# Order of the moving columns and start addresses of the matmul operands in a two-layer encoder kernel

## Chip, cores and metric

The kernel runs on one NeuronCore of one Trainium2 chip. The metric is the device time of one execution in microseconds. Two executions of the kernel before the change took 1149.13 and 1155.57 us; their median is 1152.35 us.

## What is computed

The reference is a bidirectional encoder of two layers on one sequence of 256 tokens with 1024 channels, all in float32. One layer, with the parts that this case does not touch left out:

```python
h = x + 0.5 * swiglu(rms_norm(x, norm_ffn1[i]), w_ffn1_in[i], w_ffn1_out[i])     # 1024 -> 2 x 2816 -> 1024
u = rms_norm(h, norm_mix[i])
q, k, v, c, g = jnp.split(u @ w_in[i], splits, axis=-1)                           # 512, 128, 128, 1024, 2048
y_attn = window_attention(q, k, v, sink[i], rel_bias) @ w_attn_out[i]
...
y_conv = c @ w_conv_out[i]
g_attn, g_conv = jnp.split(jax.nn.sigmoid(g), 2, axis=-1)
h = h + (g_attn * y_attn + g_conv * y_conv) @ w_o[i]
h = h + 0.5 * swiglu(rms_norm(h, norm_ffn2[i]), w_ffn2_in[i], w_ffn2_out[i])
x = h + (p[i] @ w_pe_proj[i]) * jax.nn.sigmoid(rms_norm(h, norm_pe[i]) @ w_pe_gate[i])
```

Nearly all of the arithmetic is in the matrix products with the weights. The rms norms scale each token, so the kernel multiplies the unscaled activations with the weights and scales the product afterwards.

## The kernel before

**Layout.** Activations are kept with channels on the 128 partitions and the 256 tokens along the free dimension: an activation of 1024 channels is a tile `[128, 8, 256]`, one row of 256 tokens (1024 bytes of a partition) for each group `k` of 128 channels. The result of a product is again channels by tokens, so that the weights are the stationary operand (128 x 128, loaded by a LDWEIGHTS, row "PEld" in the profile) and the 256 tokens are the moving one.

**Three products for one.** To keep float32 accuracy with the `float32r` type of the matmul, each operand is held as a pair: a part `hi`, rounded to `float32r`, and a part `lo`, what the rounding left. `mm3` (lines 309 to 317) adds three matmuls for each `k` into one PSUM tile: weight hi by activation hi (line 315), weight hi by activation lo (line 316), weight lo by activation hi (line 317). Each is one LDWEIGHTS of 128 columns and one matmul of 256 columns. `mm3` serves every product with a weight but five: keys and values (lines 676 to 678) and queries (lines 720 to 722) have it the other way round, with 128 tokens of `u` as the stationary operand and 256 or 512 columns of the weight tile as the moving one; the two output projections of attention and convolution (line 852) are plain float32 matmuls, each of which shows as two records in the trace; attention itself has its own.

**Weights.** `Weights` loads blocks of up to 1 MB from HBM into four buffers `raw` (SP's queue, line 76), and cuts them into pieces of at most 128 x 1024. For each piece ScalarE writes `w_hi` (line 100) and VectorE writes `w_lo` (line 101). Both come from one pool, `w_pool` (line 145), with seven buffers each, and `get` prepares up to six pieces ahead (line 132).

**Where things lie.** Pools lie behind one another in each partition of SBUF in the order of their creation: constants, the raw buffers, the weight tiles, a gap of 64 bytes (`gap0`, line 146), the activations (`xp`), temporary tiles, another gap of 64 bytes, and then, opened and closed as the layers go, the pool of a feed-forward stage or of the mixer. All tiles of the weight pool are 4096 bytes and those of the activations are 8192 or 22528, all multiples of 256. In the laid-out program all fourteen weight tiles begin at a multiple of 256 bytes and all activations that `mm3` reads (`x`, `xe`, `h`, `ym`, the transposed `p`) begin 64 bytes beyond one. `new_x` (line 341) makes the pair of an activation; it is reused under the tags `xah` and `xal`, so that x0, xm0, xf0, xn0, xm1 and xf1 stand in the same place one after the other.

**Order of the work.** For each layer `l`, in order: `ffn` (first feed-forward; `gate_up` 22 times, PSUM tile `ps_gu`, moving operand x; then `down` eight times, `ps_fo`, moving operand `h`), `mix` (`conv_in`, `ps_c`; keys and values, `ps_kv`; queries, `ps_q`; `conv_in` again; `gates`, `ps_g`, moving operand xm; attention, put between the gates; `attn_out` and `conv_out`, `ps_ao` and `ps_co`; `mix_out`, `ps_wo`, moving operand `ym`), `ffn` again (moving operands xf and `h`), and `embed` (`ps_pp` and `ps_pe`, moving operand `xe`). The order of the instructions on each engine comes from the framework's scheduler, by priorities; the groups of one PSUM tile follow one another on TensorE, and their evacuations follow on VectorE and ScalarE a group later (`group`, `flush`).

## Time and profile before

| what | value |
|---|---|
| two executions | 1149.13 and 1155.57 us |
| span of the profiled execution | 1155.8 us |
| TensorE matmul busy | 98 % of the span |
| TensorE weight load busy | 95 % |
| VectorE, ScalarE, GpSimd busy | 70 %, 53 %, 8 % |
| DMA queue of SP | 201.60 MB, 52.9 % of 16 engines' time |
| granted TensorE clock | 1.000 |

The profiled execution is one more execution; its span of 1155.8 us is from the first to the last instruction, and no time from outside is given for it. It lies 3.4 us above the median of the two timed ones. Matmuls are pipelined: one of 256 columns lasts some 280 ns by its record while the next one begins after less than half of that. So "busy" tells only that TensorE always had a matmul under way. What counts is the **pitch**: the time from the start of one matmul to the start of the next. It is read from a timeline (two starts and the number of matmuls between them) or from a count of matmuls in a stretch of time. In a count by windows, a matmul that is under way at either edge is counted too, so that the pitch is the stretch plus the length of one record, divided by the count.

### The profile page before, as it was taken

How to read it: one execution, taken by the hardware profiler on the slowest of the kernel's cores; microseconds unless marked ns; L12 is line 12 of the kernel's file. 1: busy time of each engine (PE TensorE's matmuls, PEld its weight loads, DVE VectorE, ACT ScalarE, POOL GpSimd, SP SyncE). 2: the span in 40 equal slices, each digit the busy share in tenths (PEclk: the TensorE clock that was granted, in tenths of full speed). 3: DMA queues.
4: the chain of work that ended last, by engine and by line, in shares of the span. 5: the costliest groups of instructions: out<-in, count | busy, mean ns of one | idle time of the engine just before them, and what ended most of it. 6: DMA issues, size and time to landing. Idle time of an engine off the chain costs nothing.

```text
span 1155.8 us, 21813 instructions
## 1 busy us (share of the span) xinstructions
PE 1136.7 (98%) x9082; PEld 1100.9 (95%) x9082; DVE 812.1 (70%) x1214; ACT 610.4 (53%) x1029; POOL 88.8 (8%) x123
## 2 busy tenths in 40 slices
PE   7999999999989999999999999999999999999998
PEld 7999999998879999999999999999987899999997
DVE  5866656798767766656886666669986686666564
ACT  6644444676346544444664444457753564444443
POOL 3000001211002000001110000113000010000110
PEclk9999999999999999999999999999999999999999
DMA  8866556545074565546556464566522664644541
GB/s 256 265 236 213 170 176 208 182 149 138 8 254 157 187 215 168 179 166 219 188 177 204 162 207 156 171 218 197 143 77 65 227 228 152 214 163 149 200 147 37
DMA packets 195695, 203.00 MB, mean 176 GB/s; under 512 B 3731, under 2 KB 188899, under 8 KB 195596
## 3 DMA queue, kind: packets, MB, share of 16 engines
q1 hardware_dynamic: 195564, 201.60, 52.9%
q8 instruction: 71, 1.16, 0.4%
q14 instruction: 28, 0.23, 0.1%
q10 hardware_dynamic: 32, 0.01, 0.0%
HBM read 200.53 MB, written 1.06 MB: 174 GB/s over the span
## 4 chain that ended last, share of the span: by engine, by line
PE 95%; DMA 2%; DVE 2%; ACT 1%; issue 0%; SPq 0%; ACTq 0%; DVEq 0%
PE ps_gu L317 14%; PE ps_gu L315 14%; PE ps_gu L316 14%; PE ps_fo L315 7%; PE ps_fo L317 7%; PE ps_fo L316 7%; PE ps_g L315 3%; PE ps_g L317 3%; PE ps_g L316 3%; PE ps_ao L852 2%; DMA raw<-in_w_o_dram 2%; PE ps_s L760 1%; PE ps_wo L316 1%; PE ps_c L315 1%; PE ps_pe L317 1%; PE ps_c L317 1%
## 5 line engine op out<-in xcount | busy, mean ns | idle before, releaser
L101 DVE TENSOR_TENSOR w_lo<-raw,w_hi 128x1024 fp32r<-128x1024 f32 (+1 forms) x368 | 441.6, 1204 | 227.8 <-ACT w_hi L100 225.9
L100 ACT CAST w_hi<-raw 128x1024 fp32r<-128x1024 f32 (+1 forms) x368 | 377.8, 1032 | 411.6 <-PE ps_gu L316 207.5
L315 PE MATMUL ps_fo<-h_hi,w_hi 128*128 128x256 f32 x704 | 196.1, 279 | 0.0
L316 PE MATMUL ps_fo<-h_lo,w_hi 128*128 128x256 f32 x704 | 195.9, 279 | 0.0
L317 PE MATMUL ps_fo<-h_hi,w_lo 128*128 128x256 f32 x704 | 195.9, 279 | 0.0
L317 PEld LDWEIGHTS ps_fo<-h_hi,w_lo 128*128 128x128 f32 x704 | 131.8, 188 | 0.0
L315 PEld LDWEIGHTS ps_fo<-h_hi,w_hi 128*128 128x128 f32 x704 | 131.8, 188 | 0.0
L316 PEld LDWEIGHTS ps_fo<-h_lo,w_hi 128*128 128x128 f32 x704 | 131.7, 187 | 0.0
L404 POOL TENSOR_TENSOR sq_acc<-sq_acc,sq 128x256 f32<-128x256 f32 x56 | 56.9, 1015 | 887.0 <-ACT sq L403 886.5
L315 PE MATMUL ps_gu<-x0h,w_hi 128*128 128x256 f32 x352 | 99.4, 282 | 2.0 <-ACT x L460 2.0
L612 DVE SCALAR_TENSOR_TENSOR y<-cpad,cw,y 128x256 f32<-128x256 f32 x240 | 101.2, 477 | 0.1
L317 PE MATMUL ps_gu<-x0h,w_lo 128*128 128x256 f32 x352 | 99.4, 282 | 0.2 <-DVE w_lo L101 0.2
L316 PE MATMUL ps_gu<-x0l,w_hi 128*128 128x256 f32 x352 | 98.9, 281 | 0.0
L315 PE MATMUL ps_gu<-xf0h,w_hi 128*128 128x256 f32 x352 | 98.6, 280 | 0.0
L315 PE MATMUL ps_gu<-xf1h,w_hi 128*128 128x256 f32 x352 | 98.6, 280 | 0.0
L316 PE MATMUL ps_gu<-xn0l,w_hi 128*128 128x256 f32 x352 | 98.5, 280 | 0.0
L315 PE MATMUL ps_gu<-xn0h,w_hi 128*128 128x256 f32 x352 | 98.4, 280 | 0.0
L316 PE MATMUL ps_gu<-xf0l,w_hi 128*128 128x256 f32 x352 | 98.4, 280 | 0.0
L316 PE MATMUL ps_gu<-xf1l,w_hi 128*128 128x256 f32 x352 | 98.4, 280 | 0.0
L317 PE MATMUL ps_gu<-xf0h,w_lo 128*128 128x256 f32 x352 | 98.3, 279 | 0.0
L317 PE MATMUL ps_gu<-xf1h,w_lo 128*128 128x256 f32 x352 | 98.3, 279 | 0.0
L317 PE MATMUL ps_gu<-xn0h,w_lo 128*128 128x256 f32 x352 | 98.2, 279 | 0.0
(225 smaller groups left out, 2677.8 us busy)
## 6 DMA issues: line engine op xcount, KB each, us to landing
raw<-in_w_ffn_in_dram SPq DMA_DIRECT2D x86, 1024.0 KB
raw<-in_w_in_dram SPq DMA_DIRECT2D x30, 1024.0 KB
raw<-in_w_ffn_out_dram SPq DMA_DIRECT2D x32, 896.0 KB
raw<-in_w_ffn_out_dram SPq DMA_DIRECT2D x16, 1024.0 KB
raw<-in_w_o_dram SPq DMA_DIRECT2D x8, 1024.0 KB
raw<-in_w_pe_gate_dram SPq DMA_DIRECT2D x8, 1024.0 KB
raw<-in_w_attn_out_dram SPq DMA_DIRECT2D x8, 512.0 KB
raw<-in_w_conv_out_dram SPq DMA_DIRECT2D x4, 1024.0 KB
```

What stands on the lines that cost most here:

```text
L100: nc.scalar.copy(out=hv[:, :, d0 : d0 + w], in_=src),
L101: nc.vector.tensor_tensor(out=lv[:, :, d0 : d0 + w], in0=src, in1=hv[:, :, d0 : d0 + w].bitcast(F32), op=ALU.subtract,),
L315: nc.tensor.matmul(ps, wh[:, k0 + k, cols], xh[:, kx, :], start=f, stop=False)
L316: nc.tensor.matmul(ps, wh[:, k0 + k, cols], xl[:, kx, :], start=False, stop=False)
L317: nc.tensor.matmul(ps, wl[:, k0 + k, cols], xh[:, kx, :], start=False, stop=e)
L404: nc.gpsimd.tensor_tensor(out=self.acc, in0=self.acc, in1=sq, op=ALU.add)
L612: nc.vector.scalar_tensor_tensor(out=y[:, i, :], in0=src, scalar=w, in1=y[:, i, :], op0=ALU.mult, op1=ALU.add)
L760: nc.tensor.matmul(ps[:, c, :], qT[v * HD : (v + 1) * HD, c, qb * P : (qb + 1) * P], kT[v * HD : (v + 1) * HD, :], start=True, stop=True,)
L852: nc.tensor.matmul(ps[:, c * T : (c + 1) * T], w[:, k, c * P : (c + 1) * P], x[:, k, :], start=k == 0, stop=k == KC - 1,)
```

## The change

Two things are changed, both in what addresses TensorE reads and in what order.

**Order.** `mm3` passes the moving rows and the PSUM tile through a view, `order.cols`. The view `plain` leaves them as they are. The view `by_halves` takes the 256 columns as two halves of 128 and reads four columns of the first half, four of the second, the next four of the first, and so on; the result is written to PSUM in the same order, so each column lands where it did. The halves lie 512 bytes apart. `by_halves` is set in `down` of the first feed-forward of both layers, in `gate_up` of the second feed-forward of both layers, in the gates of layer 1 and in `mix_out` of layer 0. Everywhere else the order is plain.

**Addresses.** The weight tiles get pools of their own for hi and lo, and each tile is eight columns (32 bytes) longer than its data, so that the seven buffers of either begin at 0, 32, 64, 96, 128, 160 and 192 bytes modulo 256. Small gap tiles (32 bytes each) part the pools. An activation tile is eight columns longer too, and its data begin at 0, 2, 4 or 6 columns (0, 8, 16 or 24 bytes) into it: x0 at 0, xm0 at 2, xf0 at 0, xn0 at 4, xm1 at 0, xf1 at 4, `xe` at 6, `h` at 0, 2, 4 and 6 in the four feed-forward stages. By the sizes of the tiles, activations hi and lo begin 64 and 96 bytes beyond a multiple of 256 for x, and 128 and 160 for a tile pair at the start of a feed-forward's pool, plus these columns.

The number of instructions of every kind stays the same, but for two memsets of gap tiles at the start.

```diff
+W_STEP = 8
...
-            hi = self.w_pool.tile([P, KD * P], F32R, name="w_hi")
-            lo = self.w_pool.tile([P, KD * P], F32R, name="w_lo")
+            hi = self.hi_pool.tile([P, KD * P + W_STEP], F32R, name="w_hi")
+            lo = self.lo_pool.tile([P, KD * P + W_STEP], F32R, name="w_lo")
...
-    w_pool = ctx.enter_context(tc.tile_pool(name="w_pool", bufs=W_BUFS))
+    hi_pool = ctx.enter_context(tc.tile_pool(name="hi_pool", bufs=W_BUFS))
+    gap2 = ctx.enter_context(tc.tile_pool(name="gap2", bufs=1))
+    lo_pool = ctx.enter_context(tc.tile_pool(name="lo_pool", bufs=W_BUFS))
+    gap3 = ctx.enter_context(tc.tile_pool(name="gap3", bufs=1))
     gap0 = ctx.enter_context(tc.tile_pool(name="gap0", bufs=1))
...
+    for gap in (gap2, gap3):
+        nc.gpsimd.memset(gap.tile([P, W_STEP], F32, name="gap"), 0.0)
...
+    def by_halves(v):
+
+        return v.rearrange("p (b a c) -> p a b c", b=2, c=4)
...
     def mm3(ps, w, x, first=True, last=True, k0=0, x_k0=0, n_k=None, cols=slice(0, P)):
         (wh, wl), (xh, xl) = w, x
+        view = order.cols
+        ps = view(ps)
...
-            nc.tensor.matmul(ps, wh[:, k0 + k, cols], xh[:, kx, :], start=f, stop=False)
-            nc.tensor.matmul(ps, wh[:, k0 + k, cols], xl[:, kx, :], start=False, stop=False)
-            nc.tensor.matmul(ps, wl[:, k0 + k, cols], xh[:, kx, :], start=False, stop=e)
+            nc.tensor.matmul(ps, wh[:, k0 + k, cols], view(xh[:, kx, :]), start=f, stop=False)
+            nc.tensor.matmul(ps, wh[:, k0 + k, cols], view(xl[:, kx, :]), start=False, stop=False)
+            nc.tensor.matmul(ps, wl[:, k0 + k, cols], view(xh[:, kx, :]), start=False, stop=e)
...
-    def new_x(tag, name):
-        return (
-            xp.tile([P, KD, T], F32R, name=name + "h", tag=tag + "h"),
-            xp.tile([P, KD, T], F32R, name=name + "l", tag=tag + "l"),
-        )
+    def rows(pool, k, name, off, **kw):
+        t = pool.tile([P, k * T + 8], F32R, name=name, **kw)
+        return t[:, off : off + k * T].rearrange("p (k t) -> p k t", t=T)
+
+    def new_x(tag, name, off):
+        return tuple(rows(xp, KD, name + part, off, tag=tag + part) for part in "hl")
...
-    def ffn(hp, l, x_in, stat_in, gain_name, xn, stat, hooks):
...
+    def ffn(hp, l, x_in, stat_in, gain_name, xn, stat, hooks, h_off, up_cols, down_cols):
+        h = tuple(rows(hp, KF, "h_" + part, h_off) for part in ("hi", "lo"))
+        order.cols = up_cols
...
+        order.cols = down_cols
         for f in range(KD):
             down(f)
         flush_urgent()
+        order.cols = plain
...
+            order.cols = by_halves if l == 1 else plain
             for i in range(0, 2 * KD, 2):
                 gates(i)
...
+            order.cols = by_halves if l == 0 else plain
             mix_out(0, 2)
             for f in range(2, KD):
                 mix_out(f, 1)
             flush_urgent()
+            order.cols = plain
...
-            ffn(hp, l, x_cur, st, "norm_mix", xn, stat, hooks)
+            ffn(hp, l, x_cur, st, "norm_mix", xn, stat, hooks, 4 * l, plain, by_halves)
...
-            ffn(hp, l, x_cur, st, "norm_pe", xe, stat, {0: lambda: embed_load(l), 4: lambda: embed_input(hp)})
+            ffn(hp, l, x_cur, st, "norm_pe", xe, stat, {0: lambda: embed_load(l), 4: lambda: embed_input(hp)}, 2 + 4 * l, by_halves, plain)
```

## The prediction, made before the result was known

> **What bounds the kernel now.** I read the page first, then the list of TensorE's waits, then stretches of the large stages and the timeline around one stage of another form. The page:

> ```profile
> span 1155.8 us, 21813 instructions
> ...
> PE 1136.7 (98%) x9082; PEld 1100.9 (95%) x9082; DVE 812.1 (70%) x1214; ACT 610.4 (53%) x1029; POOL 88.8 (8%) x123
> ...
> PE 95%; DMA 2%; DVE 2%; ACT 1%; issue 0%; SPq 0%; ACTq 0%; DVEq 0%
> ```

> TensorE holds 95% of the chain that ends last. Its waits, longest first:

> ```profile
> PE ps_yc L893 <- DVE yn L883: 3.7, 2, 1.9
> PE ps_par L196 <- DMA rows_first<-in_norm_ffn_dram: 3.3, 1, 3.3
> ```

> Even the longest sums to 3.7 us, so neither the weights nor the other engines hold TensorE up. The time is the number of matmuls by their pitch (start to start). The number, from the groups kept apart by form; each row has twins of the same count for the two other lines of `mm3`:

> ```profile
> L315 PE MATMUL ps_fo<-h_hi,w_hi 128*128 128x256 f32 x704 | 196.1, 279 | 0.0
> L315 PE MATMUL ps_gu<-x0h,w_hi 128*128 128x256 f32 x352 | 99.4, 282 | 2.0 <-ACT x L460 2.0
> L315 PE MATMUL ps_gu<-xf0h,w_hi 128*128 128x256 f32 x352 | 98.6, 280 | 0.0
> L315 PE MATMUL ps_gu<-xf1h,w_hi 128*128 128x256 f32 x352 | 98.6, 280 | 0.0
> L315 PE MATMUL ps_gu<-xn0h,w_hi 128*128 128x256 f32 x352 | 98.4, 280 | 0.0
> L315 PE MATMUL ps_g<-xm0h,w_hi 128*128 128x256 f32 x128 | 36.8, 287 | 0.0
> L315 PE MATMUL ps_g<-xm1h,w_hi 128*128 128x256 f32 x128 | 36.8, 287 | 0.0
> L315 PE MATMUL ps_pe<-xe_h,w_hi 128*128 128x256 f32 x128 | 36.5, 286 | 0.0
> L315 PE MATMUL ps_wo<-ym_h,w_hi 128*128 128x256 f32 x128 | 35.1, 282 | 0.5 <-ACT ym_h L448 0.5
> L315 PE MATMUL ps_c<-xm1h,w_hi 128*128 128x256 f32 x64 | 18.1, 282 | 0.0
> L315 PE MATMUL ps_c<-xm0h,w_hi 128*128 128x256 f32 x64 | 18.0, 282 | 0.0
> L315 PE MATMUL ps_pp<-pT_h,w_hi 128*128 128x256 f32 x32 | 8.9, 280 | 0.0
> ```

> The counts sum to 704 + 4 x 352 + 4 x 128 + 2 x 64 + 32 = 2784, by three lines 8352 of the 9082 matmuls. Their pitch, from one stretch of `ps_gu` and one of `ps_fo` (time, then busy time and count on TensorE and its weight load):

> ```profile
> 600.00:640.00 40.00, 40.00 (x342) 40.00 (x341) 4.84 (x7) 1.00 0.56 187
> 170.00:200.00 30.00, 30.00 (x257) 30.00 (x256) 1.70 (x4) 1.00 0.64 218
> ```

> With one record's length (0.28 us) added for the matmuls at the edges, 40.28 / 342 = 117.8 ns and 30.28 / 257 = 117.8 ns. Two stages with other operands agree. 8352 x 117.8 ns is 984 us of the 1155.8, and each nanosecond of this pitch is worth 8.35 us. The clock stands at 1.00 in both.

> The decisive view is the timeline of the keys and values, queries and output projection (start, length, form):

> ```profile
> 214.37 0.28 PE L676 MATMUL ps_kv<-w_hi,xm0h 128*128 128x256 f32 x1
> ...
> 219.35 0.28 PE L678 MATMUL ps_kv<-w_hi,xm0l 128*128 128x256 f32 x1
> ...
> 219.69 0.40 PE L721 MATMUL ps_q<-w_lo,xm0h 128*128 128x512 f32 x1
> ...
> 230.43 0.40 PE L722 MATMUL ps_q<-w_hi,xm0l 128*128 128x512 f32 x1
> ...
> 309.17 3.62 PE L852 MATMUL ps_ao<-o,raw 128*128 128x256 f32 x16
> ...
> 312.63 0.60 PE L874 MATMUL ps_yt<-ident,y 128*128 128x128 f32 x4
> ```

> Of `ps_kv`, 44 matmuls lie between the two starts: 4.98 / 44 = 113.2 ns. These have the same form as those of `mm3`: 128 columns loaded, 256 moved, into a row of 256 in PSUM. What differs is which operand is which: here the weight tile moves (at 0 modulo 256 bytes) and the activation is loaded (at 64), there the reverse. So the same form has been seen 4.6 ns apart, with places in memory as the plainest difference. The queries, 46 intervals in 10.74 us, take 233.5 ns for 512 columns. The float32 projection has 16 records in 3.62 us: (3.62 - 0.38) / 15 = 216 ns. The transposes, (0.60 - 0.27) / 3 = 110 ns, are the shortest pitch here with 128 columns loaded for every matmul.

> **The reordered stages.** They hold 1056 matmuls of `ps_fo` (half of 2112), 2112 of `ps_gu` (xf0 and xf1), 384 of `ps_g` (xm1) and 192 of `ps_wo` (half of 384): 3744. The other 4608 stay plain. No row shows a moving row read in two halves, so I bound it. My picture of the 4.6 ns: the moving stream passes 256 columns in about the time that the next weight load takes for 128, so it goes through the places modulo 256 bytes twice as fast and meets the weight load on its way. Reading four columns of each half in turn, with halves 512 bytes apart, it goes through them at the weight load's own pace and keeps its distance. The best then is the transposes' 110 ns, -7.8 x 3744 = -29.2 us. From above, a stream that waited for every load would run at the projection's 216 ns, +98 x 3744 = +368 us; that is far from a picture in which the two run side by side. I take the keys' 113.2 ns, the nearest row in form and the lowest that any pair of weight load and 256 columns shows: -4.6 x 3744 = **-17.2 us**.

> [...]

> **The plain stages.** Their weight tiles now begin at seven places 32 bytes apart, and the activations at several. Two relations are known: +64 (117.8) and -64 (113.2). If the mean over places is that of these two rows, 115.5, the 4608 gain 2.3 x 4608 = 10.6 us; if +64 was a middling place, nothing; if it was a good one, a loss as large, +10.6. With one row of this very kind at 117.8 I take half of the gain, **-5.3 us**. The 192 matmuls of keys and queries change places too: at 4.6 ns, 0.9 us at most, left out.

> **The other engines.** They write and read the shifted tiles. The convolution's taps read at every multiple of 4 bytes over 31 places:

> ```profile
> L612 DVE SCALAR_TENSOR_TENSOR y<-cpad,cw,y x240: 391/478/486, 219.4 to 880.7; 128x256 f32<-128x256 f32 x120
> ...
> L100 ACT CAST w_hi<-raw 128x1024 fp32r<-128x1024 f32 x304 | 317.5, 1051 | 330.5 <-PE ps_gu L316 188.2 <-PE ps_fo L316 68.9 <-PE ps_g L316 18.4
> L101 DVE TENSOR_TENSOR w_lo<-raw,w_hi 128x1024 fp32r<-128x1024 f32 x304 | 371.6, 1228 | 170.0 <-ACT w_hi L100 168.1 <-DMA rows_late<-in_q_norm_dram 1.8
> L556 DVE TENSOR_TENSOR gu<-ps_gu,r_x 128x512 f32<-128x512 f32 x88 | 60.6, 690 | 27.3 <-PE ps_gu L317 27.0
> L562 DVE TENSOR_TENSOR hh<-sg,gu 128x256 f32<-128x256 f32 x88 | 36.7, 419 | 0.8 <-ACT sg L560 0.8
> L449 DVE TENSOR_TENSOR h_lo<-hh,h_hi 128x256 fp32r<-128x256 f32 x88 | 36.8, 420 | 4.2 <-ACT h_hi L448 4.2
> ...
> L153 POOL MEMSET gap<- 128x16 f32 x2 | 0.2, 111 | 0.0
> ```

> Median 478 and maximum 486 ns show no place that is dear, so I put this at nothing. Does the supply of weights keep up? A pair of pieces feeds 48 matmuls, 48 x 113.2 = 5.43 us; VectorE needs 2 x 1.23 for it and 0.69 + 0.42 + 0.42 for the evacuation, 3.99 us in all. ScalarE is idle before its pieces for 330 us because TensorE still holds the buffers: cover that lasts, and without it each late piece would cost its 1.05 + 1.23 us. If every place at which these engines begin cost a tenth more, VectorE would need 4.4 us, still under 5.43. Two more memsets of 0.1 us each lie on GpSimd ahead of TensorE's first work, which waits 3.3 us for a load (row above): nothing.

> **The sum.** 1155.8 - 17.2 - 5.3 = 1133.3 us for the profiled execution. Its span is 3.4 us above the median of 1152.35, so for the median: 1152.35 - 22.5 = **1129.9 us**, 2.0% less. Its own range is 1119 to 1141: at the low end the reordered stages halfway to 110 ns (-23.2) and the plain ones at -10.6, at the high end a third of the reordered gain missing (-11.5) and the plain ones as they were.

> **Rivals.**

> *Places don't matter.* The 4.6 ns may come from the operands' roles, a fixed time of the weight load for instance. Then the order is as good as free and the time stays at 1152, 1145 to 1159. For it: `ps_gu` and `ps_fo` agree to 0.1 ns over seven buffers of either kind. Against: those all lie at one place modulo 256 bytes, so their agreement tests nothing, and nothing else differs in form from `ps_kv`. [...] The 113.2 against 117.8 of two equal forms speaks against it without deciding.

> *More than forecast.* The distance is kept everywhere and the plain stages find better places too: 110 ns for 3744 and 115.5 for 4608, -29.2 - 10.6 = -39.8, 1112.6 us. For it: the projection, which moves columns at half the pace, has one pitch over 16 records and nothing in it that looks like a wait. Against: no load of this type with 256 columns has been seen under 113.2.

> *Slower: streams in step stay together.* If the two run at one pace, a pair that begins at the same place collides along the whole row and not twice. The weight tiles begin at seven places, so for about one buffer in seven every line waits, and the pitch there is the projection's 216 ns: 98 x 3744 / 7 = +52.4; the other six sevenths gain 14.7. That gives 1152.35 + 37.7 = 1190 us. It makes the kernel 2% slower once a colliding pair costs over 70 ns (14.7 us to win back and 23 us on top, over 535 matmuls). Against it: a load that has waited once is behind and should no longer meet.

> *Slower: each jump costs.* A row in halves has 64 jumps on the reading and the writing side, the PSUM side above all. At one column's time per jump (117.8 / 256 = 0.46 ns), 29 ns a matmul, +110 us, 1262 us. From 0.10 ns per jump (23 us / 3744 / 64) it is slower by 2%. No row speaks for or against it, since every output of `mm3` is contiguous now. [...]

> **How the numbers follow.** Forecast 0.38, more 0.20, places don't matter 0.18, in step 0.16, jumps 0.08. About 2% is what a measurement of this kernel can tell from no change: 1129.3 and 1175.4 us are the borders. The forecast lies on the first, half on either side. Faster: 0.20 + 0.19 = 0.39. Slower: 0.16 + 0.08 + 0.01 = 0.25. Within: 0.36. The range runs from the case of more, with the plain stages still better (113.2 would give 21 us in place of 10.6), 1102, to the case in step with a little above, 1195; outside are the jumps and some 0.05 at either end.

> **What would show it.** Right: in stretches of `ps_fo` of the first feed-forward and of `ps_gu` of the second a pitch near 113 ns, and in the plain stages between 113 and 118, changing from piece to piece as the buffers change. Wrong: a pitch of 117.8 everywhere (places don't matter); in the reordered stages, pieces at 113 with every seventh far above (in step); an even rise in all reordered stages, whatever the buffer (jumps). TensorE's list of waits should stay as it is; a wait for w_lo or w_hi in it would refute the paragraph on supply.

## The result, and the profile after

The changed kernel takes **1201.43 us** (two executions, 1200.91 and 1201.96) against 1152.35 before: 4.3% slower, ratio 1.0426 with an interval of 1.0299 to 1.0553. The forecast was 1129.9 us with a range up to 1195; the sign was wrong and the time lies outside the range. The interval is that wide because the two runs of before lie 6.4 us apart; thirteen later runs of it have a median of 1156.23 us (1150.47 to 1157.66).

The page of the kernel after, the same lines as of before, and from its groups the two that supply the weights and one of TensorE (busy us and mean ns of one behind the first bar):

```profile
span 1199.1 us, 21818 instructions
...
PE 1182.4 (99%) x9082; PEld 1147.1 (96%) x9082; DVE 812.0 (68%) x1214; ACT 614.5 (51%) x1029; POOL 88.1 (7%) x125
...
PE 97%; DMA 1%; DVE 1%; ACT 1%; issue 0%; ACTq 0%; DVEq 0%
...
L101 ACT CAST w_hi<-raw 128x1024 fp32r<-128x1024 f32 (+1 forms) x368 | 381.0, 1040 | 450.3 <-PE ps_gu L334 227.9
L102 DVE TENSOR_TENSOR w_lo<-raw,w_hi 128x1024 fp32r<-128x1024 f32 (+1 forms) x368 | 441.3, 1204 | 248.1 <-ACT w_hi L101 246.1
...
L333 PE MATMUL ps_gu<-xf0h,w_hi 128*128 128x256 f32 x352 | 103.1, 293 | 0.0
```

The number of matmuls is the same, VectorE is busy for the same 812 us, and ScalarE, before its pieces of weights, is idle for 450.3 us in place of the 411.6 on the page of before; what ends most of that idle time is TensorE (`<-PE ps_gu` in the row), which gives the buffers back later. The longest wait of TensorE by line is the same 3.7 us:

```profile
PE ps_yc L913 <- DVE yn L903: 3.7, 2, 1.9
```

So the 43.3 us between the spans are pitch. The groups hide it: a record of `xf0h` is only 13 ns longer than before. The pitch is read from stretches of one stage. In such rows come the stretch, its length, then busy time and count on TensorE, on its weight load and on VectorE, the granted clock, the DMA share and GB/s; the pitch is the length plus one record (0.28 or 0.29 us) by the count of TensorE. `ps_gu` of the kernel after, a reordered stage (xf0) and a plain one (xn0):

```profile
400.00:500.00 100.00, 100.00 (x780) 100.00 (x779) 11.07 (x16) 1.00 0.50 166
620.00:720.00 100.00, 100.00 (x849) 100.00 (x847) 12.43 (x18) 1.00 0.54 183
```

and `ps_fo`, reordered (layer 0, first feed-forward) and plain (second), where `h` begins 8 bytes beyond a multiple of 16:

```profile
140.00:200.00 60.00, 60.00 (x467) 60.00 (x466) 2.98 (x7) 1.00 0.51 168
512.00:572.00 60.00, 60.00 (x501) 60.00 (x500) 2.97 (x7) 1.00 0.56 191
```

Reordered: 100.29 / 780 = 128.6 ns and 60.29 / 467 = 129.1 ns, where before had 117.8. Plain: 118.1 and 120.3. Taken stage by stage from the starts of the matmuls, the 3744 reordered ones have a mean of 128.5 (127.9 to 129.2): +10.7 x 3744 = **+40 us**. The plain ones are 0.2 to 2.6 ns up, weighted by their counts **+6 us**. Together 46, against 43.3 of the spans. The clock is 1.00, as before.

### The profile page after: what moved, and what is told of

The parts are those of the page before. It is cut to its first block, busy times and chain, and to the rows that moved or that the text cites. A ratio compares the mean times of both kernels' runs of the same rounds, so it can differ in the third digit from the quotient of the medians.

```text
span 1199.1 us, 21818 instructions
## 1 busy us (share of the span) xinstructions
PE 1182.4 (99%) x9082; PEld 1147.1 (96%) x9082; DVE 812.0 (68%) x1214; ACT 614.5 (51%) x1029; POOL 88.1 (7%) x125
## 4 chain that ended last, share of the span: by engine, by line
PE 97%; DMA 1%; DVE 1%; ACT 1%; issue 0%; ACTq 0%; DVEq 0%
PE ps_gu L335 15%; PE ps_gu L334 14%; PE ps_gu L333 14%; PE ps_fo L335 7%; PE ps_fo L333 7%; PE ps_fo L334 7%; PE ps_g L333 3%; PE ps_g L335 3%; PE ps_g L334 3%; PE ps_ao L872 2%; PE ps_wo L334 1%; PE ps_s L779 1%; PE ps_wo L335 1%; PE ps_pe L333 1%; PE ps_c L333 1%; PE ps_c L334 1%
## 5 line engine op out<-in xcount | busy, mean ns | idle before, releaser
L101 ACT CAST w_hi<-raw 128x1024 fp32r<-128x1024 f32 (+1 forms) x368 | 381.0, 1040 | 450.3 <-PE ps_gu L334 227.9
L102 DVE TENSOR_TENSOR w_lo<-raw,w_hi 128x1024 fp32r<-128x1024 f32 (+1 forms) x368 | 441.3, 1204 | 248.1 <-ACT w_hi L101 246.1
L335 PE MATMUL ps_fo<-h_hi,w_lo 128*128 128x256 f32 x704 | 202.3, 288 | 0.0
L333 PE MATMUL ps_fo<-h_hi,w_hi 128*128 128x256 f32 x704 | 202.1, 288 | 0.0
L334 PE MATMUL ps_fo<-h_lo,w_hi 128*128 128x256 f32 x704 | 201.8, 288 | 0.0
L335 PE MATMUL ps_gu<-xf0h,w_lo 128*128 128x256 f32 x352 | 103.5, 294 | 0.0
L334 PE MATMUL ps_gu<-xf0l,w_hi 128*128 128x256 f32 x352 | 103.3, 294 | 0.0
L335 PE MATMUL ps_gu<-xf1h,w_lo 128*128 128x256 f32 x352 | 103.3, 294 | 0.0
L333 PE MATMUL ps_gu<-xf0h,w_hi 128*128 128x256 f32 x352 | 103.1, 293 | 0.0
L333 PE MATMUL ps_gu<-xf1h,w_hi 128*128 128x256 f32 x352 | 103.0, 293 | 0.0
L334 PE MATMUL ps_gu<-xf1l,w_hi 128*128 128x256 f32 x352 | 102.9, 292 | 0.0
```

Of the source, the lines that this page charges most:

```text
L101: nc.scalar.copy(out=hv[:, :, d0 : d0 + w], in_=src),
L102: nc.vector.tensor_tensor(out=lv[:, :, d0 : d0 + w], in0=src, in1=hv[:, :, d0 : d0 + w].bitcast(F32), op=ALU.subtract,),
L333: nc.tensor.matmul(ps, wh[:, k0 + k, cols], view(xh[:, kx, :]), start=f, stop=False)
L334: nc.tensor.matmul(ps, wh[:, k0 + k, cols], view(xl[:, kx, :]), start=False, stop=False)
L335: nc.tensor.matmul(ps, wl[:, k0 + k, cols], view(xh[:, kx, :]), start=False, stop=e)
```

## The experiments

Two theories stood at the beginning. *Order*: the loss comes from the order of the columns, on the reading or the writing side. *Places*: it comes from where the operands now begin, and the order only shows it. The first four kernels part the change. Times are medians beside the runs of before on the same chip (1156.23 us for these four). Where only one run was made, the text says so. A pitch "from the starts" is the mean interval between the starts of matmuls that follow each other in one stage, without the intervals that hold a pause. The code is shown shortened, and `AT` and `ORDER` stand in a short form.

### The two halves of the change

**Addresses alone** (the kernel after, without the order):

```diff
-ffn(..., 4 * l, plain, by_halves)
+ffn(..., 4 * l, plain, plain)
-ffn(..., 2 + 4 * l, by_halves, plain)
+ffn(..., 2 + 4 * l, plain, plain)
...
-order.cols = by_halves if l == 1 else plain
+order.cols = plain
```

> The new addresses alone, every stage in plain order. Theory 'jump' (every jump of the reading or writing order costs, wherever the tiles lie): the plain stages of the changed kernel run at 118 to 120 ns, so this takes 1155 to 1163 us. Theory 'in step' (a moving row read at the weight load's pace collides with it where both begin at the same place): addresses alone cost nothing, 1149 to 1156 us. Rival 'addresses' (the many places are the whole loss): 1190 to 1200 us.

1163.67 us, ratio 1.0073 (1.0046 to 1.0099). `ps_fo` of the first and of the second feed-forward of layer 0, with `h` at a multiple of 16 bytes and 8 bytes beyond one:

```profile
150.00:190.00 40.00, 40.00 (x340) 40.00 (x339) 2.12 (x5) 1.00 0.65 218
500.00:540.00 40.00, 40.00 (x335) 40.00 (x333) 2.28 (x6) 1.00 0.57 192
```

40.28 / 340 = 118.5 and 40.28 / 335 = 120.2 ns. The new addresses cost 7.4 us on their own, most of it where rows begin 8 bytes off. That is far from the 1190 to 1200 us of the rival *addresses*: they are not the whole loss.

**Order alone** (the kernel before, with the order in the same stages):

```diff
 (wh, wl), (xh, xl) = w, x
+view = order.cols
+ps = view(ps)
...
-nc.tensor.matmul(ps, wh[:, k0 + k, cols], xh[:, kx, :], start=f, stop=False)
+nc.tensor.matmul(ps, wh[:, k0 + k, cols], view(xh[:, kx, :]), start=f, stop=False)
```

> The new order alone, in the same stages as in the changed kernel, with all tiles at their old addresses (weights at 0, activations at 64 modulo 256 bytes). 'Jump': the reordered 3744 matmuls at 127 to 130 ns, +35 to +45 us, 1187 to 1198 us. 'In step': at this one distance of 64 bytes the streams keep apart, so 113 to 118 ns and 1135 to 1153 us. 'Addresses': 1152 us.

1188.67 us, ratio 1.0287 (1.0262 to 1.0312). `ps_gu`, reordered and plain:

```profile
400.00:480.00 80.00, 80.00 (x634) 80.00 (x633) 8.99 (x13) 1.00 0.55 182
620.00:720.00 100.00, 100.00 (x852) 100.00 (x851) 12.27 (x18) 1.00 0.53 178
```

126.6 and 117.7 ns. *In step* gave 113 to 118 ns for this place and falls there. The order alone costs 8.9 ns x 3744 = 33 us at the old addresses, where every weight tile begins at 0 and every activation at 64 modulo 256 bytes. The two halves of the change make 7.4 + 32.4 = 40 us; both together make 45 against the 1156.23 of these runs. The 5 that are left go with the order at the new places, 128.5 instead of 126.7: 1.8 x 3744 = 7 us.

**Reading alone** (as the one before, without `ps = view(ps)`) and **writing alone** (with it, and without the views of xh and xl):

> As the new order alone, but only the reading of the moving rows goes by halves; PSUM is written in plain order, so the tokens of these stages end up in other columns. If the cost of the jump is on the reading side (SBUF), 1187 to 1198 us as with both; if on the writing side (PSUM), 1149 to 1156 us. 'In step' expects what it expects of the order alone, 1135 to 1153 us, since the reading is the same.

> As the new order alone, but only the writing of PSUM goes by halves and the moving rows are read in plain order, so the tokens of these stages end up in other columns. If the cost is on the writing side, 1187 to 1198 us; if on the reading side, 1149 to 1156 us. 'In step' expects 1149 to 1156 us.

Reading alone: 1189.53 us, ratio 1.0297 (1.0266 to 1.0327); its `ps_gu` in the stage of xf0:

```profile
400.00:480.00 80.00, 80.00 (x634) 80.00 (x633) 8.99 (x13) 1.00 0.54 179
```

Writing alone: 1155.79 us, ratio 1.0003 (0.9982 to 1.0023); its `ps_gu` in the stages of x0, not touched by the edit, and of xf0, written in halves:

```profile
60.00:130.00 70.00, 70.00 (x620) 70.00 (x620) 9.00 (x13) 1.00 0.59 200
400.00:480.00 80.00, 80.00 (x682) 80.00 (x681) 9.85 (x15) 1.00 0.52 176
```

and its `ps_fo`, first feed-forward, written in halves:

```profile
140.00:190.00 50.00, 50.00 (x443) 50.00 (x443) 2.97 (x7) 1.00 0.55 186
```

Reading has the same count of 634 in the same 80 us as the whole order. Writing has 117.7 in `ps_gu`: writing by halves costs nothing. But 70.28 / 620 = 113.4 and 50.28 / 443 = 113.5 are a surprise. The stage of x0 has the code and the addresses of before, where the same stretch has

```profile
60.00:130.00 70.00, 70.00 (x597) 70.00 (x596) 8.99 (x13) 1.00 0.60 203
```

70.28 / 597 = 117.7 there and 113.4 here: equal matmuls at equal addresses have two steady paces. The last section comes back to it.

### The places

**All activations at 192** (before, with a longer gap ahead of them; weights stay at 0):

```diff
-for gap in (gap0, gap1):
-    nc.gpsimd.memset(gap.tile([P, 16], F32, name="gap"), 0.0)
+for gap, n in ((gap0, 48), (gap1, 16)):
+    nc.gpsimd.memset(gap.tile([P, n], F32, name="gap"), 0.0)
```

> The kernel before, with one gap longer by 128 bytes, so that all activations that mm3 reads lie at 192 modulo 256 bytes in place of 64, in plain order; the weights stay at 0. Theory 'place' (as predicted: the keys' 113.2 ns come from their distance of -64 bytes): mm3 at 113 to 114 ns, 1112 to 1125 us. Theory 'pace' (TensorE falls into one of two steady paces, 113 or 118 ns, after each interruption and keeps it; the writing-only run had both in one stage at one place): mostly 118 ns as before, 1145 to 1158 us, and if a stage has 113 it is another one than the place alone would say. 'Roles': 1152 us with the keys still at 113 ns.

**1125.38 us**, ratio 0.9739 (0.9708 to 0.977): faster than both kernels. Its page, then `ps_gu` (xf0) and `ps_fo`:

```profile
span 1124.2 us, 21813 instructions
...
PE 1103.4 (98%) x9082; PEld 1068.5 (95%) x9082; DVE 811.4 (72%) x1214; ACT 610.6 (54%) x1029; POOL 88.6 (8%) x123
```

```profile
400.00:460.00 60.00, 60.00 (x532) 60.00 (x532) 7.61 (x11) 1.00 0.56 190
```

```profile
140.00:190.00 50.00, 50.00 (x443) 50.00 (x443) 2.55 (x6) 1.00 0.58 197
```

113.3 and 113.5 ns. The feed-forward stages have 113.3 to 113.5 and `ps_wo` 113.4 in both layers; `ps_g` stays at 116.2 and 114.7. The keys and values, where the operands are exchanged, go the other way, from 113.6 to 117.9. The two paces don't explain this gain: by the theory *pace* most stages would have stayed at 118, but all feed-forward stages have the faster pitch, and the four runs lie between 1123.39 and 1126.05 us. (All tiles behind the gap move by 128 bytes, not the moving operands alone.)

**One place for each stage** (plain order; `rows` puts the data of each activation at a place of its own; ha and hb are `h` of the first and the second feed-forward):

```diff
+def rows(pool, k, name, at):
+    off = (at - 64) % 256 // 4
+    t = pool.tile([P, k * T + 64], F32R, name=name)
+    return t[:, off : off + k * T].rearrange("p (k t) -> p k t", t=T)
+AT = {"x0": 0, "ha0": 32, "xm0": 96, "xf0": 128, "hb0": 160, "xe0": 192, "xn0": 224,
+      "ha1": 16, "xm1": 112, "xf1": 144, "hb1": 176, "xe1": 208}
```

> Plain order, weights at 0, and each of twelve stages with its activations at another place modulo 256 bytes, all multiples of 16 (0, 16, 32, 96, 112, 128, 144, 160, 176, 192, 208, 224). 'Place': the stages differ, the one at 192 near 113 ns, others between 113 and 122. 'Pace': every stage at 113 or 118 ns, nothing between, with no order in the places. Both: 1140 to 1160 us.

1162.43 us, one run. `ps_gu` at 0, 128, 224 and 144, in this order of the rows:

```profile
60.00:130.00 70.00, 70.00 (x586) 70.00 (x585) 8.30 (x12) 1.00 0.60 200
400.00:480.00 80.00, 80.00 (x677) 80.00 (x676) 9.95 (x15) 1.00 0.55 182
600.00:700.00 100.00, 100.00 (x847) 100.00 (x847) 11.75 (x17) 1.00 0.57 189
960.00:1060.00 100.00, 100.00 (x845) 100.00 (x845) 11.76 (x17) 1.00 0.54 180
```

119.9, 118.6, 118.4 and 118.7 ns. From the starts, for the other stages: 16: 116.7; 32: 117.8; 96: 119.9; 112: 114.5; 160: 117.3; 176: 119.3; 192: 113.4 to 115.0; 208: 119.2. So the place is worth up to 6.6 ns, 64 is a middling one, and the mean of these twelve and 64 is 117.9: nothing was to be had by spreading. Most of these values are neither 113.3 nor 117.8, so the two paces alone don't make them. Keys and values show that the place of the loaded operand counts too: their moving weight tiles stay at 0, and with the loaded activation at 96 and 112 they take 118.5 and 120.1, at 64 they took 113.6.

**All rows 8 bytes further** (`x`, `xe` and `h` at 72 instead of 64):

```diff
-AT = {"x0": 0, "ha0": 32, ...}
+AT = dict.fromkeys(AT, 72)
```

> The kernel before in plain order with the activations of x, xe and h 8 bytes further on (72 in place of 64 modulo 256), so that a row no longer begins at a multiple of 16 bytes; weights at 0. In the run with the new addresses alone the stages of this kind ran at 120 to 121 ns and the others at 118. [...] Theory 'mixture' (the loss in that run comes from weight tiles at many places): 1149 to 1157 us.

1186.98 us, ratio 1.0275 (1.0238 to 1.0313). `ps_gu` (xf0):

```profile
400.00:490.00 90.00, 90.00 (x742) 90.00 (x741) 10.38 (x15) 1.00 0.56 185
```

90.28 / 742 = 121.7 ns, and from the starts 120.7 to 122.0 in the other stages at 72: the 8 bytes cost 3.9 ns for each matmul at this place. *Mixture* falls: the weight tiles all lie at 0 here, and still these stages take what the stages with rows 8 bytes beyond a multiple of 16 took with the new addresses (120 to 121 ns), or a little more.

### The order

**A different order for each stage** (before, old addresses; b blocks, c columns of each in turn, read and written). In the names u is `gate_up`, d `down`, a and b the first and the second feed-forward, the digit the layer:

```diff
+def by(b, c):
+    return lambda v: v.rearrange("p (b a c) -> p a b c", b=b, c=c)
+ORDER = {"ua0": (2, 8), "da0": (2, 16), "g0": (2, 32), "ub0": (4, 4), "db0": (8, 4), "pe0": (16, 4),
+         "ua1": (32, 4), "da1": (4, 8), "g1": (2, 2), "wo1": (2, 64), "ub1": (2, 4), "pe1": (16, 8)}
```

> Old addresses; every stage in an order of its own, b parts read c columns at a time in turn. Theory 'jump' (each jump in reading costs the same, 8.9 ns over 64 jumps with b=2, c=4): 2 parts by 8 columns 122 ns, by 16 120, by 32 119, by 64 118, by 2 136; 4, 8, 16 or 32 parts by 4 columns 127; 4, 16 or 32 parts by 8 122. Theory 'same place' (a jump of 512 or 256 bytes comes back to the same place modulo 256, and only that costs): 2 and 4 parts by 4 columns 127, 8 parts (128 bytes apart) between, 16 and 32 parts (64 and 32 bytes apart) 118. Theory 'pace of the weight load' (only halves by 4 run at its pace): all others 118.

1217.97 us, one run. `ps_gu` with four blocks 256 bytes apart and with 32 blocks 32 bytes apart:

```profile
400.00:500.00 100.00, 100.00 (x740) 100.00 (x739) 10.41 (x16) 1.00 0.50 164
640.00:720.00 80.00, 80.00 (x686) 80.00 (x685) 10.34 (x15) 1.00 0.56 189
```

and `ps_fo` with two blocks by 16 columns, eight by 4, four by 8, and plain:

```profile
155.00:200.00 45.00, 45.00 (x377) 45.00 (x376) 2.12 (x5) 1.00 0.59 200
525.00:575.00 50.00, 50.00 (x397) 50.00 (x396) 2.55 (x6) 1.00 0.56 189
745.00:790.00 45.00, 45.00 (x369) 45.00 (x368) 2.13 (x5) 1.00 0.60 199
1125.00:1170.00 45.00, 45.00 (x385) 45.00 (x384) 2.55 (x6) 1.00 0.59 199
```

With four columns at a time: two blocks (512 bytes apart) 126.7, four (256) 135.5, eight (128) 126.7, sixteen (64) 115.4 in `ps_pp` and 116.3 in `ps_pe`, thirty-two (32) 117.0. All of these change the block at every step, so *jump* falls, and only those cost that come back to the same place modulo 256 bytes, at once or at every second step. *Same place* had this right in kind, but gave 127 for four blocks. With two blocks 512 bytes apart the cost falls with the number of changes: 126.7, 123.4, 120.0, 119.2 and 118.0 for runs of 4, 8, 16, 32 and 64 columns. Runs of two columns take 170.0; which side of the matmul pays for them, the reading or the writing, wasn't tried apart. With runs of eight columns, four blocks take 122.9 and sixteen 118.2 in `ps_pp` and 119.1 in `ps_pe`.

**Other distances** (reading only: two blocks by four columns at a distance d other than 512 bytes; tokens are read twice or left out; d is 480 and 448 bytes in `gate_up` of xf0 and xf1, 384 and 496 in `down`, 416 in the gates, and 512 in `mix_out`):

```diff
+def apart(d, b=2, c=4):
+    return lambda v: bass.AP(v.tensor, v.offset, [list(v.ap[0]), [c, 256 // b // c], [d, b], [1, c]])
...
-nc.tensor.matmul(ps, wh[:, k0 + k, cols], xh[:, kx, :], start=f, stop=False)
+nc.tensor.matmul(ps, wh[:, k0 + k, cols], view(xh[:, kx, :]), start=f, stop=False)
```

> Reading only, in the stages of the reordered set, four columns in turn from two blocks of 128 columns that lie a given distance apart; PSUM is written in plain order and all else lies as before. Where the distance is under 512 bytes the blocks overlap, so that some tokens are read twice and the last ones left out; every matmul still moves 256 columns with 64 jumps. Second feed-forward's gate_up: 480 bytes apart in layer 0, 448 in layer 1; first feed-forward's down: 384 and 496; gates of layer 1: 416; mix_out of layer 0: 512, as in the changed kernel. Theory 'same place' (a jump costs where it comes back to the same place modulo 256 bytes): 113 to 119 ns everywhere but in mix_out, which has 127; 1150 to 1165 us. Theory 'far jump' (any jump of 128 bytes or more costs, 32 and 64 are free): 125 to 129 ns in all of them, 1185 to 1195 us.

1172.92 us, one run. `ps_gu` in the stage of x0 (plain), of xf0 (480 bytes) and of xf1 (448):

```profile
60.00:130.00 70.00, 70.00 (x620) 70.00 (x619) 8.99 (x13) 1.00 0.59 203
400.00:480.00 80.00, 80.00 (x651) 80.00 (x650) 8.99 (x13) 1.00 0.52 170
960.00:1060.00 100.00, 99.80 (x817) 99.61 (x816) 11.76 (x17) 1.00 0.55 183
```

123.3 at 480 and 122.5 at 448 (in this row 0.2 us of gap are taken off), and from the starts 123.3 at 384 and 496, 121.0 at 416, 126.7 at 512 (`ps_wo`). Leaving the 512 bytes takes 3.4 to 5.7 ns off; another 3.2 to 5.5 over the plain 117.8 stay at every distance. So neither theory holds as it stands: *same place* gave 113 to 119 and *far jump* 125 to 129. The plain stage of x0 again runs at 113.4.

**More blocks at other distances** (reading only, the same edit): four blocks of 4 columns 240 and 208 bytes apart (`ps_gu`, xf0 and xf1), eight 112 bytes apart, and two by 8 columns 480 bytes apart (`ps_fo`, layers 0 and 1); four blocks 224 bytes apart in the gates of layer 1, and two by 8 columns 64 bytes apart in `mix_out` of layer 0. *Pace*: a stream that goes through the places at a quarter of the pace is dear by itself. *Far jump*: each change of block costs by its distance.

> Reading only, at the old addresses, from blocks that lie at distances that are no multiple of 256 bytes, tokens read twice or left out as in the run on distance. Four blocks by 4 columns, 240 bytes apart (second gate_up of layer 0), 208 (of layer 1), 224 (gates of layer 1); eight blocks 112 bytes apart (first down of layer 0); two blocks by 8 columns, 480 bytes apart (first down of layer 1) and 64 bytes apart (mix_out of layer 0). Theory 'pace' (what is left of the halves' cost at such distances, 3 to 5 ns, comes from the row going through the places at half its pace beside the weight load; a quarter is worse): 126 to 134 for four blocks. Theory 'far jump' for that part (each jump of over 64 bytes costs a little): 121 to 124 for four and eight blocks, half of the excess, 119 to 121, for two blocks by 8 columns, 480 apart, and 118 for 64 apart.

1162.46 us, one run. `ps_gu`, then `ps_fo`, then `ps_wo` (64 bytes):

```profile
390.00:480.00 90.00, 90.00 (x773) 90.00 (x773) 11.06 (x17) 1.00 0.56 185
950.00:1050.00 100.00, 99.81 (x836) 99.62 (x835) 11.76 (x17) 1.00 0.57 187
```

```profile
150.00:200.00 50.00, 50.00 (x419) 50.00 (x418) 2.55 (x6) 1.00 0.60 201
715.00:765.00 50.00, 50.00 (x407) 50.00 (x407) 2.89 (x7) 1.00 0.55 182
```

```profile
345.00:364.00 19.00, 19.00 (x158) 19.00 (x157) 2.41 (x6) 1.00 0.52 171
```

Four blocks at 240 bytes take 116.8 ns, as little as the plain order; at 208 bytes it is 119.7, at 224 from the starts 119.3, eight blocks at 112 bytes 120.0. Both theories gave more than that for four blocks (126 to 134, and 121 to 124), and both are refuted. Four blocks at 256 bytes took 135.5, but that pair is not clean: there PSUM was written in four blocks too, and that writing costs nothing was shown for halves alone. How much of the 19 ns the sixteen bytes of distance are worth is therefore not shown.

Two by 8 columns take 123.3 from the starts at 480 bytes and 121.6 at 64, where *far jump* gave 119 to 121 and 118. The 123.3 is what two by 4 columns took at 480 bytes, with twice the jumps, and what two by 8 took at 512 bytes (123.4). So the extra cost of the 512 bytes was seen with runs of four columns and not with runs of eight.

### Order and place together

**Halves and 8 bytes at other places** (read and written; `ORDER` and `AT` as above). *Separate terms*: the order costs its 8.9 and the 8 bytes their 3.9, wherever. *One cause*: only the distance to the weight tile counts, and both merely shift it.

```diff
+AT = {"x0": 200, "ha0": 192, "xm0": 200, "xf0": 192, "hb0": 200, "xe0": 200, "xn0": 192,
+      "ha1": 0, "xm1": 112, "xf1": 128, "hb1": 8, "xe1": 40}
+ORDER = {"da0": (2, 4), "ub0": (2, 4), "ua1": (16, 4), "da1": (2, 4), "g1": (2, 4), "ub1": (2, 4)}
```

> Weights at 0 modulo 256 bytes; by stage, plain rows 8 bytes past places measured before (200 in the first gate_up, the mixer of layer 0 up to its gates, the second down and the embedding of layer 0; 8 in the last down; 40 in the last embedding), halves read in turn at 192 (first down and second gate_up of layer 0), 0 (first down of layer 1), 112 (gates of layer 1) and 128 (last gate_up), and sixteenths at 192 (first gate_up of layer 1). [...] Theory 'one cause' (only the distance to the weight tile counts, and 8 bytes or another order merely shift it): 200 between its neighbours 192 (113.4) and 208 (119.1), and halves near 113 at one place at least.

1192.94 us, one run. `ps_gu` of xn0, sixteen blocks at 192, and `ps_fo` with halves at 192, halves at 0, plain at 8:

```profile
620.00:710.00 90.00, 90.00 (x789) 90.00 (x789) 11.07 (x16) 1.00 0.58 195
```

```profile
150.00:200.00 50.00, 50.00 (x397) 50.00 (x396) 2.55 (x6) 1.00 0.54 180
730.00:780.00 50.00, 50.00 (x398) 50.00 (x396) 2.55 (x6) 1.00 0.53 179
1100.00:1150.00 50.00, 50.00 (x427) 50.00 (x426) 2.98 (x7) 1.00 0.59 200
```

Halves take 126.6 and 126.3 in these rows and from the starts 126.7 at 192 and 0, 126.8 at 112, 129.5 at 128: nearly the same wherever the plain order has 113.4, 119.9, 114.5 and 118.6. They don't add a fixed sum to the place; they bring every place to 126.7 or more. The 8 bytes aren't a fixed sum either: plain at 8 has 117.8 where 0 had 120.0, at 200 it has 120.1 where 192 had 113.4, at 40 it has 119.2 where 32 had 117.8. *Separate terms* fell. So did *one cause*: 200 doesn't lie between its neighbours (113.4 and 119.2), and halves are near 113 nowhere.

**Two blocks 480 bytes apart at twelve places** (reading only). *In step*: the 3 to 5.5 ns that stay with two blocks are collisions with the weight load and change with the place, as the prediction's rival had it. *Two blocks*: they belong to the order and are the same everywhere.

```diff
+view = apart(120)
+AT = {"x0": 0, "ha0": 32, ...}
```

> Reading only, in every product of mm3, four columns in turn from two blocks 480 bytes apart (tokens read twice or left out), with the twelve stages at the twelve places of the run on places (0, 16, 32, 96, 112, 128, 144, 160, 176, 192, 208, 224 modulo 256 bytes). Theory 'in step' (two blocks go through the places at the weight load's pace, and what is left of the cost is their lasting meeting): the stages differ by the place, some at 113 to 118 ns and others at 123 to 130. Theory 'two blocks' (the part that is left belongs to the order itself): 121 to 125 ns at every place.

1195.42 us, one run. `ps_gu` at 0, `ps_fo` at 32 and at 16:

```profile
60.00:130.00 70.00, 70.00 (x578) 70.00 (x577) 8.31 (x12) 1.00 0.57 193
```

```profile
150.00:200.00 50.00, 50.00 (x411) 50.00 (x411) 2.55 (x6) 1.00 0.53 180
740.00:790.00 50.00, 50.00 (x419) 50.00 (x419) 2.55 (x6) 1.00 0.58 195
```

121.6, 122.3 and 120.0; all stages by their starts lie between 120.0 and 123.4, without any of the places standing out that are good or bad in the plain order. *In step* is refuted for the places tried; *two blocks*, which gave 121 to 125, holds within 1 ns.

**Sixteen blocks everywhere** (read and written; `by(16, 4)` in all of `mm3`, the places of `AT` as first given):

> Every product of mm3 reads four columns of each of 16 parts in turn (64 bytes apart), with each of twelve stages at another place modulo 256 bytes, the same twelve places as in the run on places. Theory 'same place': no stage pays for its jumps, 110 to 122 ns by the place, the best stages under the 113.3 that plain order reached at 192; 1130 to 1160 us. Theory 'far jump': the same, since 64 bytes are free there. If the order mattered and the place did not, all stages would lie at the 116 ns that this order had at 64: 1135 to 1142 us.

1133.8 us, one run (before on that chip 1157.64). `ps_gu` at 0 and at 128:

```profile
60.00:130.00 70.00, 70.00 (x620) 70.00 (x620) 8.99 (x13) 1.00 0.59 201
380.00:470.00 90.00, 89.81 (x783) 89.64 (x783) 11.76 (x17) 1.00 0.56 185
```

113.4 at 0, where the plain order took 119.9, and 90.09 / 783 = 115.1 at 128, where it took 118.6. From the starts all stages lie between 113.6 and 116.7 but one (144: 117.9). An order with 64 jumps for each row can be better than the plain one. The single place 192 with the plain order is still ahead, 1125.38 us.

## Why the prediction was wrong

**What bounds the kernel** was read rightly: waits, clock and supply stay as they were, and the time is matmuls by pitch. The paragraph on the other engines held; a `w_lo` piece is 1204 ns on the mean in both kernels when its forms are taken together, and TensorE waits for one in all 0.2 us before and after.

**The step that failed** is "I take the keys' 113.2 ns". The reordered stages measured 128.5, +10.7 in place of -4.6: +40 us in place of -17.2, a swing of 57 us, and this decides the sign. Two things were wrong in it. The picture behind it (a stream at the weight load's own pace keeps its distance), which no run shows, made the order a remedy for the place. The runs show that reading by halves costs by itself: 8.9 ns at the old addresses, with the writing side plain as with both sides, and 126.7 or more at the four other places that were tried with both sides. And the row chosen was no bound for it: 113.2 is the pitch of a plain row at a good place, so it could tell what a place is worth and nothing of an order that no row showed. The bounds of 110 and 216 ns did hold the 128.5; with no row for the operation, the value should not have been set at the favourable one.

**Where the cost of the order comes from** is shown in part. It isn't the jumps as such (sixteen blocks by four columns take 113.6 to 117.9 where the plain order takes 113.4 to 119.9), not the writing of PSUM by halves (1.0003) and not the pace through the places (four blocks at 240 bytes, a quarter of the pace, take 116.8). A part is the return to the same place modulo 256 bytes: two blocks by four columns take 126.7 at 512 bytes and 121.0 to 123.3 at other distances, all reading only. Four blocks point the same way (135.5 at 256 bytes, 116.8 at 240), but there the writing differs as well. The 3 to 5.5 ns that stay were seen with two blocks at every distance and place tried, while four blocks at 208 to 240 bytes differ from plain by -1 to +2 ns. Why two blocks cost this, and why two at 512 bytes cost less than four at 256, stays open.

**The plain stages** were put at -5.3 us and came to +6. The step "if the mean over places is that of these two rows" was the favourable one of three named; "a middling place, nothing" was right, since thirteen places average 117.9. What the prediction did not have is the 8 bytes: it costed activations that begin 0, 8, 16 or 24 bytes into their tile alike, and in the kernel after those at 8 modulo 16 took 120.2 where the others took 118.2. Its sign that the pitch changes with the buffers came true on a small scale: in the stage of xn0 the pieces go from 117.7 to 119.2 ns and repeat every seven.

**The rivals.** *Each jump costs* described what the profile would show (an even rise in all reordered stages, whatever the buffer) and 10.7 / 64 = 0.17 ns for each jump lies above the 0.10 from which it makes the kernel 2% slower, though far under the 0.46 that it was reckoned with. Its place was wrong: that it named PSUM above all was a guess that no run shows, and writing by halves, in runs of four float32 columns, costs nothing (ratio 1.0003). Nor does each jump cost, as the sixteen blocks show (113.6 to 117.9 ns). *In step* gave 1190 us, near the result, by a mechanism that the runs refute: in the kernel after, the pieces of the reordered `ps_gu` lie between 125 and 131 ns and repeat every seven, as the buffers do, with none near 113 and none far above; and two blocks at 480 bytes take 120.0 to 123.4 at every place. *Places don't matter* is refuted by the 1125.38 us against 1156.15 of before on that chip, since only places in memory differ there. That the distance between the two operands counts fits keys and values at first, which go from 113.6 to 117.9 where `mm3` goes from 117.8 to 113.3. With the activation at 96 and 112 they take 117.5 to 118.9 and 119.6 to 120.1 in three runs, where `mm3` at the same distances (160 and 144) takes 117.3 and 118.7. So the fit is good to some 1.5 ns, and no run tries the distance by itself.

**The trace's hint** was half right. 113.2 against 117.8 for equal forms did point to a faster pitch that places can reach in all of `mm3`. But the change didn't put the operands there.

## What to carry to other kernels

A stage bound by back-to-back matmuls is read by its pitch, since its busy share and the length of its records hardly move (here 98 to 99% and 280 to 293 ns where the pitch went from 117.8 to 128.6). The cheapest thing to try is one gap ahead of the moving operands, the same offset to the weight tiles for all of them (here 128 bytes more, 2.6%), and not a spread over many places, which gave their mean here. Begin rows at multiples of 16 bytes: of four places 8 bytes beyond one, three were dearer than the place 8 bytes lower, by 1.4 to 6.7 ns, and one was cheaper by 2.2. Don't read blocks by four columns in turn where they lie 128, 256 or 512 bytes apart (126.7, 135.5 and 126.7 ns here), and don't take the duration of a plain row in another stage as the price of an access pattern that no row shows.
